# One input array in six transfers, the norm's weight folded into its scaling, and centering queued behind scaling, in a two-layer encoder

## The chip, the cores and the metric

The kernel runs on one core of one Trainium2 chip. The metric is the device time of that core in microseconds (us), launch to end. The median of three runs of the kernel before is 1676.47 us (1676.05 to 1679.31). Five engines work side by side and wait for each other through semaphores: PE (matmuls), DVE (vector), ACT (scalar), POOL (GpSimd) and SP, which here only issues transfers.

## The reference

Two layers on 256 tokens (272 in layer 0, with 16 learned tokens ahead) of width D = 1024, each a token mixer and a product-key expert layer, each followed by a residual sum and a layer norm:

```python
x = layer_norm(alpha * x + rglru_mixer(x))      # layer 0: x @ w_in, conv of 4 taps, gates, two scans, w_out
x = layer_norm(alpha * x + peer_ffn(x))
x = layer_norm(alpha * x + conformer(x))        # layer 1: pw1, GLU, conv of 31 taps, layer_norm, silu, pw2
x = layer_norm(alpha * x + peer_ffn(x))

def layer_norm(x, g, b):
    mu = mean(x); var = mean((x - mu) ** 2)
    return (x - mu) * rsqrt(var + eps) * g + b

def peer_ffn(x):                                # q = x @ w_query, top 16 of 2 x 128 keys, 16 experts of 16384
    ...                                         # weighted sum of expert rows peer_v by gelu(peer_u . x)
```

## The kernel before

**Layout.** Activations lie feature-major: a tile [128, 8, n] holds the 1024 features in 8 blocks of 128 partitions, n tokens along the free axis (n is 272 in layer 0 and 256 in layer 1). Weights come from memory in blocks of 512 KB, [128, 1024], into a ring "raw" of four buffers and at times a fifth (`stream`, `load` at L159, issued on SP's queue in program order; a counter `turn["raw"]`, modulo 5, says whose turn it is). For most products a weight block is split into a rounded high part (ACT, L172) and the rest (DVE, L181), and so are the activations; `linears` then makes three products for each block: high by high, low weight by high activation (on PE "u<-xs,lo"), and high weight by low activation. The first two blocks of a call can be held together (`defer=2`): for each k both units do the two products that need the activation's high part only, and the products that need its low part come last. `linears_whole` (L276) multiplies unsplit float32.

**The start.** `run` ends its setup with seven matmuls on a constant (L135, "idle"). `recurrent` (L466) then brings x and the first two blocks of w_in in eight transfers (L474 halves of a weight block, 256 KB; L478 quarters of x, 272 KB), then the parameter columns `par` (L480), one more block of w_in, and four blocks of gate weights (L506). The first two products (L608) run in halves of k: four k of unit 0, four of unit 1, and again. `gates(b)` makes the convolution of unit b on DVE (L508, then three L512), `uc`; PE multiplies it by the gate weights (L525, L527); meanwhile PE does the third unit of w_in (L276). Small DVE operations (L660 and others, "spl") make a softplus of 128x16 beside it.

**The norms.** `normed` (L399) is a generator: sums for mean and variance by matmuls with a constant matrix; centering x - mu on DVE (L405), 8 blocks; rstd by an ACT estimate and one Newton step of three DVE operations (L433 to L435), each of which needs the one before; scaling by rstd (L441), 8 blocks, each yielded to the caller. If products were made ahead (`self.pre` set), all 8 blocks are centered ahead of rstd; otherwise four are, and the other four are queued no earlier than L435. The norm inside the conformer (tile cy, 256 tokens) is the one of the second kind that the change touches; ACT applies weight, shift and silu (L1390), PE multiplies the first two weight blocks by cy unsplit (L223), and DVE splits cy for the rest (L1395, L1396).

**The norm ahead of the expert layer.** `norm_split` (L451), used once in each layer, writes for each block the high part `hi` = round(y*g + b) (ACT L457 for six blocks, POOL L455 for k = 2 and 5), then y = y*g + b in place (L462, six on DVE, two on POOL), then `lo` = y - hi (L463, DVE), and after blocks 3 and 7 a transfer of four blocks of y to memory ("saved", L671, on SP's queue). `peer` then takes the query products: q is written from two products made ahead (ACT L699) and from PSUM (DVE L701), in a tile that reuses the memory of x, so the first of these writes wait until "saved" has been read out of it. The products run over a ring of PSUM banks (0, 1, 2, 7, 6).

The order of the instructions on each engine is the program's, with a scheduler that places them by readiness; `issue_after(i)` holds an instruction of the same engine behind i.

## Time and profile before

| | |
|---|---|
| median of three runs | 1676.47 us (1676.05 to 1679.31) |
| profiled execution | 1678.47 us, span 1676.7 us, mean granted clock 0.998 |
| busy: PE, DVE, ACT, POOL | 1660.4, 1493.8, 1056.3, 744.1 us |
| PE's part of the chain that ended last | 94% |
| moved from and to memory | 449 MB, 268 GB/s over the span |

The profiled execution is 1.77 us longer than its span and 2.0 us above the median. A row of the timeline gives the start in us from the start of the span, the time from the first start to the last end of a group, the engine, the line, the operation with what it writes and reads, the number of instructions, and in brackets the idle time ahead of it with what ended it. Rows are modelled to overlap by a latency: eight matmuls of 0.23 us each take 2.00 us as a row, and the next row starts 1.83 us after the first.

### The profile page before, as it was taken

Reading aid. Unit: us, or ns where it says so; the run is one execution under the profiler, and the core shown is the slowest. Engines: PE = TensorE matmul, PEld = TensorE weight load, DVE = VectorE, ACT = ScalarE, POOL = GpSimd, SP = SyncE. Lnnn points to the kernel's source line nnn. Section 1 sums busy time; section 2 is a strip of 40 time slices with the busy share of each in tenths; the row PEclk is TensorE's granted clock in tenths of the full one; section 3 lists DMA queues with packets and bytes.
Section 4 is the critical chain, followed back from the end, with each engine's and each line's share of the span. In section 5 each row is a group of like instructions: output and inputs, shape, how many; then the busy total and the mean of one; then the engine's idle time right before and its main releaser. Section 6 shows DMA issues by size and latency. Waiting matters only on the chain.

```text
span 1676.7 us, 34167 instructions
## 1 busy us (share of the span) xinstructions
PE 1660.4 (99%) x12640; PEld 1609.8 (96%) x12640; DVE 1493.8 (89%) x2839; ACT 1056.3 (63%) x2024; POOL 744.1 (44%) x549
## 2 busy tenths in 40 slices
PE   9999999999999999999999999999999999999997
PEld 7999999999999999999989899999999999999997
DVE  6996999899998888988789969989899998899896
ACT  6754545578776555786567645456788875555552
POOL 0001873343453677753059017733333226777530
PEclk9999999999999999999999999999999999999999
DMA  6546679988777999999732355699888879999994
GB/s 214 176 158 172 201 222 357 315 287 282 258 263 238 350 345 354 347 357 333 272 113 89 126 178 185 210 320 335 289 290 269 280 239 354 356 374 362 366 369 159
DMA packets 135640, 451.17 MB, mean 269 GB/s; under 512 B 23472, under 2 KB 24624, under 8 KB 135344
## 3 DMA queue, kind: packets, MB, share of 16 engines
q1 hardware_dynamic: 98016, 324.66, 57.0%
q0 software_dynamic: 37456, 124.33, 20.2%
q8 instruction: 99, 1.62, 0.4%
q14 instruction: 69, 0.57, 0.1%
HBM read 437.10 MB, written 11.82 MB: 268 GB/s over the span
## 4 chain that ended last, share of the span: by engine, by line
PE 94%; DVE 4%; ACT 1%; issue 1%; DMA 0%; DVEq 0%; SPq 0%; ACTq 0%
PE u L215 32%; PE acc L935 20%; PE acc L939 13%; PE u L254 10%; PE u L257 5%; PE u L276 5%; PE g L841 1%; PE g L842 1%; PE cv L1518 1%; PE sps L716 1%; PE u L210 1%; PE acc L981 1%; PE u L608 1%; DVE lo L181 0%; PE pre L296 0%
## 5 line engine op out<-in xcount | busy, mean ns | idle before, releaser
L172 ACT ACTIVATE hi<-raw 128x1024 fp32r<-128x1024 f32 x559 | 592.0, 1060 | 481.9 <-PE acc L935 212.7
L181 DVE TENSOR_TENSOR lo<-raw,hi 128x1024 fp32r<-128x1024 f32 x503 | 616.4, 1227 | 98.7 <-ACT hi L172 96.5
L1270 POOL DMA_INDIRECT rows<-peer_v,ids x160 | 262.4, 1640 | 290.1 <-DVE few_out L1303 183.3
L215 PE MATMUL u<-xs,hi 128*128 128x240 f32 (+3 forms) x3056 | 385.9, 277 | 0.8 <-DVE xs L463 0.6
L935 PE MATMUL acc<-w,hi 128*128 128x384 f32 (+1 forms) x1952 | 374.1, 333 | 0.0
L215 PEld LDWEIGHTS u<-xs,hi 128*128 128x128 f32 x3056 | 364.5, 189 | 1.9 <-DVE xs L463 1.0
L935 PEld LDWEIGHTS acc<-w,hi 128*128 128x128 f32 x1952 | 320.1, 189 | 0.0
L939 PE MATMUL acc<-w,lo 128*128 128x192 f32 (+1 forms) x2016 | 261.2, 271 | 0.0
L939 PEld LDWEIGHTS acc<-w,lo 128*128 128x128 f32 x2016 | 258.8, 191 | 0.0
L215 PE MATMUL u<-xs,lo 128*128 128x240 f32 (+3 forms) x1528 | 208.8, 277 | 1.0 <-DVE lo L181 1.0
L1303 DVE SCALAR_TENSOR_TENSOR few_out<-rows,act,few_out 128x1024 f32<-128x1024 f32 x153 | 195.6, 1278 | 4.9 <-DMA rows<-peer_v,ids 4.9
L215 PEld LDWEIGHTS u<-xs,lo 128*128 128x128 f32 x1528 | 190.3, 189 | 1.5 <-DVE lo L181 1.4
L181 POOL TENSOR_TENSOR lo<-raw,hi 128x1024 fp32r<-128x1024 f32 x56 | 134.5, 2405 | 106.1 <-ACT hi L172 68.3
L254 PE MATMUL u<-xs,hi 128*128 128x448 f32 x784 | 179.5, 371 | 0.0
L1270 POOL DMA_INDIRECT rows<-u_rows,ids x64 | 88.2, 1379 | 170.7 <-DVE rows L1276 123.0
L1280 POOL DMA_INDIRECT act<-own,turn x96 | 139.9, 1458 | 40.3 <-issue 22.7
L254 PEld LDWEIGHTS u<-xs,hi 128*128 128x128 f32 x784 | 140.2, 189 | 10.3
L826 ACT ACTIVATE Bl<-AB,glT 128x128 f16<-128x128 f16 x368 | 112.8, 391 | 14.2 <-PE g L842 13.0
L257 PEld LDWEIGHTS u<-xs,lo 128*128 128x128 f32 x784 | 102.4, 191 | 3.4
L257 PE MATMUL u<-xs,lo 128*128 128x224 f32 x784 | 102.8, 273 | 0.0
L276 PE MATMUL u<-x,raw 128*128 128x272 f32 x368 | 86.6, 392 | 0.0
L276 PEld LDWEIGHTS u<-x,raw 128*128 128x128 f32 x368 | 69.9, 190 | 14.4
(332 smaller groups left out, 2016.4 us busy)
## 6 DMA issues: line engine op xcount, KB each, us to landing
raw<-peer_u SPq DMA_DIRECT2D x256, 512.0 KB, 4.7
raw<-peer_v SPq DMA_DIRECT2D x248, 512.0 KB, 6.3
raw<-w_query SPq DMA_DIRECT2D x28, 512.0 KB, 4.1
raw<-pw SPq DMA_DIRECT2D x22, 512.0 KB, 3.5
raw<-w_in SPq DMA_DIRECT2D x14, 512.0 KB, 5.2
own<-own POOLq DMA_DIRECT2D x20, 256.0 KB, 5.3
raw<-w_out SPq DMA_DIRECT2D x8, 512.0 KB, 3.3
raw<-peer_v SPq DMA_DIRECT2D x16, 256.0 KB, 4.1
```

The lines of the kernel that those rows point to most:

```text
L172: self.act_hi = nc.scalar.activation(hi, raw, AF.Copy).ins
L181: i = e.tensor_tensor(lo[:, s], raw[:, s], hi[:, s].bitcast(F32), op=OP.subtract)
L215: self.mm = nc.tensor.matmul(ps[:, :n], l[:, k, :], xs(k, r)[:, :n], start=start, stop=stop)
L254: self.mm = nc.tensor.matmul(both, hi[:, k, :], xs(k)[:, :, :n], start=k == 0, stop=k == NB - 1, skip_group_check=True)
L257: self.mm = nc.tensor.matmul(ps[:, n:2 * n], lo[:, k, :], xs(k, 0)[:, :n], start=False, stop=k == NB - 1, skip_group_check=True)
L276: self.mm = self.nc.tensor.matmul(ps[:, :n], raw[:, k, :], x[:, k, :n], start=k == 0, stop=k == NB - 1)
L826: nc.scalar.activation(Bl[:, c], Bh[:, c], AF.Copy, scale=glT[:, c0 + c:c0 + c + 1])
L935: self.mm = nc.tensor.matmul(acc[b][:, :2 * n], hi, w, start=j == 0, stop=j == NK - JG - 1, skip_group_check=True)
L939: self.mm = nc.tensor.matmul(main[b][:, :n], hi if p_ else lo, w[:, i * n:i * n + n], start=False, stop=j == NK - 1 and not p_, skip_group ...
L1270: self.last_rows = self.nc.gpsimd.indirect_dma_start(out=t, out_offset=None, in_=table, in_offset=bass.IndirectOffsetOnAxis(ap=few["ids"][ ...
L1280: self.nc.gpsimd.indirect_dma_start(out=few["act"][:, k:k + 1], out_offset=None, in_=few["lead"]["table"].rearrange("p j (t o) -> (p j t) ...
L1303: nc.vector.scalar_tensor_tensor(lead["out"], t, w, lead["out"], op0=OP.mult, op1=OP.add)
```

## The change

It has three parts.

1. **Start.** The host lays x and the first two weight blocks into one array "first", [128, 8, 272 + 256]: for each k the tokens and both units' 128 columns. Six transfers bring k = 0, 1, 2, 3 one by one (264 KB each), then 4-5 and 6-7 (528 KB each); `par` is issued ahead of the last. The two units' products follow the same bounds. The ring's counter is set to 2, so that the later loads use the same buffers as before. Five idle matmuls stand where there were seven. Gate blocks 0 and 2 are issued, then a block of w_in, then gate blocks 1 and 3. The scans write in place instead of in a tile of their own.
2. **norm_split.** The scaling multiplies by g and rstd in one operation on DVE (L443). `hi` takes only the shift and is made by ACT for all eight blocks (L457). `lo` = (y + b) - hi is one DVE operation (L461): eight where there were six and eight. y = y + b comes last and all on POOL (L464), each behind its own `lo`, and the two saving transfers behind the fourth and the eighth of these.
3. **Centering.** Where four blocks are centered after rstd, each is queued behind the scaling ahead of it instead of behind rstd.

```diff
+PARTS = (0, 1, 2, 3, 4, 6, 8)
...
-            for _ in range(7):
+            for _ in range(5):
                 nc.tensor.matmul(idle, self.ones16, self.ones16[:, None, :].to_broadcast([P, 4, P]), start=True, stop=True)
...
-    def normed(self, sp, y, n):
+    def normed(self, sp, y, n, gain=None):
...
-        i = nc.vector.scalar_tensor_tensor(r[1], r[1], 1.5, r[0], op0=OP.add, op1=OP.mult).ins
+        nc.vector.scalar_tensor_tensor(r[1], r[1], 1.5, r[0], op0=OP.add, op1=OP.mult)
         self.rstd = r[1]
         for k in range(NB):
             if k >= early:
-                with self.tc.issue_after(i):
+                with self.tc.issue_after(self.scaled):
                     center(k)
-            self.scaled = nc.vector.tensor_tensor(y[:, k, :n], y[:, k, :n], r[1], op=OP.mult).ins
+            z = y[:, k, :n]
+            self.scaled = (nc.vector.scalar_tensor_tensor(z, z, gain(k), r[1], op0=OP.mult, op1=OP.mult) if gain else
+                           nc.vector.tensor_tensor(z, z, r[1], op=OP.mult)).ins
             yield k
...
     def norm_split(self, sp, y, n, g, b, hi, lo, done):
         nc = self.nc
-        for k in self.normed(sp, y, n):
-            if k % 3 == 2:
-                nc.gpsimd.tensor_scalar(hi(k), y[:, k, :n], g(k), b(k), op0=OP.mult, op1=OP.add)
-            else:
-                i = nc.scalar.activation(hi(k), y[:, k, :n], AF.Identity, scale=g(k), bias=b(k))
-                if k == 7:
-                    self.pins.append(i.ins)
+        for k in self.normed(sp, y, n, g):
+            i = nc.scalar.activation(hi(k), y[:, k, :n], AF.Identity, bias=b(k))
+        self.pins.append(i.ins)
         for k in range(NB):
-            e = nc.gpsimd if k % 3 == 2 else nc.vector
-            e.tensor_scalar(y[:, k, :n], y[:, k, :n], g(k), b(k), op0=OP.mult, op1=OP.add)
-            nc.vector.tensor_tensor(lo(k), y[:, k, :n], hi(k).bitcast(F32), op=OP.subtract)
-            done(k)
+            z = y[:, k, :n]
+            i = nc.vector.scalar_tensor_tensor(lo(k), z, b(k), hi(k).bitcast(F32), op0=OP.add, op1=OP.subtract)
+        with self.tc.issue_after(i.ins):
+            for k in range(NB):
+                nc.gpsimd.tensor_scalar(y[:, k, :n], y[:, k, :n], b(k), None, op0=OP.add)
+                done(k)
...
+            first = sp.tile([P, NB, n + 2 * P], F32, name="first", bufs=1)
+            x = first[:, :, :n]
+            pair = [first[:, :, n + i * P:n + (i + 1) * P] for i in range(2)]
+            self.turn["raw"] = 2
+            for k, k1 in zip(PARTS, PARTS[1:]):
+                if k1 == NB:
+                    nc.sync.dma_start(self.par, a["par"])
+                nc.sync.dma_start(first[:, k:k1, :], a["first"][:, k:k1, :])
+            self.early.append(self.load(a["w_in"][0]))
...
-                    for i in range(4):
+                    for i in (0, 2, 1, 3):
+                        if i == 1:
+                            self.early.append(self.load(a["w_in"][1]))
                         nc.sync.dma_start(gw[:, i], a["gates"][i])
...
-                    h = sp.tile([P, n], F32, tag="h", name="h", bufs=4)
+                    h = t
...
-            for k0 in range(0, NB, 4):
+            for k, k1 in zip(PARTS, PARTS[1:]):
                 for t, raw in zip(ps, pair):
-                    for k in range(k0, k0 + 4):
-                        self.mm = nc.tensor.matmul(t, raw[:, k * P:(k + 1) * P], x[:, k, :], start=k == 0, stop=k == NB - 1)
+                    for i in range(k, k1):
+                        self.mm = nc.tensor.matmul(t, raw[:, i, :], x[:, i, :], start=i == 0, stop=i == NB - 1)
```

On SP's queue the kernel before starts with these transfers (x and h0, w_in's halves, par, then whole blocks):

```order
L474 DMA raw<-w_in 128x512
L478 DMA x_118<-h 128x544 x2
L474 DMA raw<-w_in 128x512 x2
L478 DMA x_118<-h 128x544 x2
L474 DMA raw<-w_in 128x512
L480 DMA par<-par 128x448
L159 DMA raw<-w_in 128x1024
L506 DMA gw<-gates 128x1024 x4
```

The changed kernel starts with these:

```order
L478 DMA first<-first 128x528 x4
L478 DMA first<-first 128x1056
L477 DMA par<-par 128x448
L478 DMA first<-first 128x1056
L160 DMA raw<-w_in 128x1024
L506 DMA gw<-gates 128x1024 x2
L160 DMA raw<-w_in 128x1024
L506 DMA gw<-gates 128x1024 x2
```

The first product needed two transfers, half a weight block and a quarter of x (528 KB), and needs one of 264 KB now; the fourth block of w_in has moved between the gate blocks.

On DVE, at the norm inside the conformer, the kernel before has this order (cy is the tile that is normed, mu its mean, L433 to L435 make rstd):

```order
L405 TENSOR_TENSOR cy<-cy,mu 128x256 x4
L433 SCALAR_TENSOR_TENSOR rstd_12104<-var,rstd_12103 128x256
L434 SCALAR_TENSOR_TENSOR rstd_12104<-rstd_12104,rstd_12103 128x256
L435 SCALAR_TENSOR_TENSOR rstd_12104<-rstd_12104,rstd_12103 128x256
L405 TENSOR_TENSOR cy<-cy,mu 128x256
L441 TENSOR_TENSOR cy<-cy,rstd_12104 128x256 x5
L405 TENSOR_TENSOR cy<-cy,mu 128x256 x2
L441 TENSOR_TENSOR cy<-cy,rstd_12104 128x256 x2
```

The changed kernel has this at the same place; the last two rows then come three times more:

```order
L406 TENSOR_TENSOR cy<-cy,mu 128x256 x4
L434 SCALAR_TENSOR_TENSOR rstd_12082<-var,rstd_12081 128x256
L435 SCALAR_TENSOR_TENSOR rstd_12082<-rstd_12082,rstd_12081 128x256
L436 SCALAR_TENSOR_TENSOR rstd_12082<-rstd_12082,rstd_12081 128x256
L444 TENSOR_TENSOR cy<-cy,rstd_12082 128x256 x4
L406 TENSOR_TENSOR cy<-cy,mu 128x256
L444 TENSOR_TENSOR cy<-cy,rstd_12082 128x256
```

No centering stands between rstd and the first scaling any more, and the later centerings alternate with the scalings of the same block.

On DVE, at the end of the norm ahead of layer 0's expert layer and at the first query products, the kernel before has this order (xs is the split activation, pre the products made ahead, lo a weight block's low part, q the queries):

```order
L462 TENSOR_SCALAR x_118<-x_118,par 128x272 x2
L463 TENSOR_TENSOR xs_1158<-x_118,xs_1158 128x272 x2
L310 COPY pre_c<-pre 128x2 x2
L312 SCALAR_TENSOR_TENSOR pre<-still,pre_c,pre 128x272 x2
L313 TENSOR_TENSOR pre<-pre,rstd_1188 128x272 x2
L181 TENSOR_TENSOR lo<-raw,hi 128x1024
L701 COPY q<-u 128x272 x2
L181 TENSOR_TENSOR lo<-raw,hi 128x1024
L701 COPY q<-u 128x272
```

The changed kernel has this, from the scaling on:

```order
L443 SCALAR_TENSOR_TENSOR first<-first,par,rstd_1166 128x272 x8
L461 SCALAR_TENSOR_TENSOR xs_1135<-first,par,xs_1135 128x272 x4
L461 SCALAR_TENSOR_TENSOR xs_1136<-first,par,xs_1136 128x272 x4
L311 COPY pre_c<-pre 128x2 x2
L313 SCALAR_TENSOR_TENSOR pre<-still,pre_c,pre 128x272 x2
L314 TENSOR_TENSOR pre<-pre,rstd_1166 128x272 x2
L182 TENSOR_TENSOR lo<-raw,hi 128x1024 x2
L701 COPY q<-u 128x272 x3
```

The six operations y*g + b have left DVE, and the first two copies to q, which wait for the saving transfers, stand behind a second weight block's low part.

More of the change, by code (lines that the diff above doesn't have):

```diff
@@ L469, in recurrent @@
         with tc.tile_pool(name="mix0", bufs=2) as sp:
-            x = sp.tile([P, NB, n], F32, name="x0", bufs=1)
-            pair = [self.stream("raw", F32, 4, None) for _ in range(2)]
-            def part(i, k):
-                nc.sync.dma_start(pair[i][:, k * P:(k + 4) * P], a["w_in"][i][:, k * P:(k + 4) * P])
-            for k in range(0, NB, 4):
-                part(0, k)
-                for k2 in (k, k + 2):
-                    nc.sync.dma_start(x[:, k2:k2 + 2, :], a["h0"][:, k2:k2 + 2, :])
-                part(1, k)
-            nc.sync.dma_start(self.par, a["par"])
-            self.early.append(self.load(a["w_in"][2]))
+            first = sp.tile([P, NB, n + 2 * P], F32, name="first", bufs=1)
[7 more added lines that the diff above has]
+            self.early.append(self.load(a["w_in"][0]))
             gw, pre_w = (sp.tile([P, 4, NB, P], F32, tag="gw", name="gw", bufs=1) for _ in range(2))
@@ L604, in recurrent @@
             ps = [self.psum("u", (0, 1, 2))[:, :n] for _ in pair]
-            for k0 in range(0, NB, 4):
+            for k, k1 in zip(PARTS, PARTS[1:]):
                 for t, raw in zip(ps, pair):
-                    for k in range(k0, k0 + 4):
-                        self.mm = nc.tensor.matmul(t, raw[:, k * P:(k + 1) * P], x[:, k, :], start=k == 0, stop=k == NB - 1)
+                    for i in range(k, k1):
+                        self.mm = nc.tensor.matmul(t, raw[:, i, :], x[:, i, :], start=i == 0, stop=i == NB - 1)
             for b in range(2):
                 gates(b, ps[b])
-            self.linears_whole([a["w_in"][b] for b in range(2, NB)], x, n, taken, (0, 1, 2))
+            self.linears_whole([a["w_in"][b] for b in range(NB - 2)], x, n, taken, (0, 1, 2))
             ring = (7, 0, 1, 2, 3, 4, 5, 6)
-            self.linears_whole([a["w_in"][NB + b] for b in range(WHOLE)], x, n, gelu, ring)
+            self.linears_whole([a["w_in"][NB - 2 + b] for b in range(WHOLE)], x, n, gelu, ring)
             self.hi_pin = last[0].ins
-            self.linears([a["w_in"][NB + b] for b in range(WHOLE, NB)], xs, n, FULL, lambda b, ps: gelu(WHOLE + b, ps), ring=ring)
+            self.linears([a["w_in"][NB - 2 + b] for b in range(WHOLE, NB)], xs, n, FULL, lambda b, ps: gelu(WHOLE + b, ps), ring=ring)
             for b in range(NB):
@@ L1681 @@
     arrays = {
-        "h0": np.ascontiguousarray(h0.reshape(T0, NB, P).transpose(2, 1, 0)),
+        "first": np.concatenate([h0.reshape(T0, NB, P).transpose(2, 1, 0),
+                                 *(w.reshape(P, NB, P) for w in w_in[NB:NB + 2])], axis=2),
         "par": np.ascontiguousarray(np.concatenate([cols(i[n]) for n, _ in _PARTS], axis=1)),
@@ L1685 @@
         "gb": np.stack([i["ln_ffn_g"][1], i["ln_ffn_b"][1]]),
-        "w_in": np.concatenate([w_in[NB:], w_in[:NB]]),
+        "w_in": np.concatenate([w_in[NB + 2:], w_in[:NB]]),
         "gates": np.ascontiguousarray(
```

## The prediction

> **What bounds the kernel now.** I read the page first, its busy times and its chain.
>
> ```profile
> span 1676.7 us, 34167 instructions
> PE 1660.4 (99%) x12640; PEld 1609.8 (96%) x12640; DVE 1493.8 (89%) x2839; ACT 1056.3 (63%) x2024; POOL 744.1 (44%) x549
> PE 94%; DVE 4%; ACT 1%; issue 1%; DMA 0%; DVEq 0%; SPq 0%; ACTq 0%
> ```
>
> PE is busy for all but 1676.7 - 1660.4 = 16.3 us, and it makes 94% of the chain. No product is removed except two idle ones, so a gain can only come out of PE's idle time at the places that the change touches. Next I read the timeline around those places: the start (four rows), then a narrow window at each norm (one row each).
>
> ```profile
> 1.14 3.17 PE L135 MATMUL idle<-ones 128*128 128x512 f16 x7 [1.14 <-POOL ones L108]
> 4.67 8.66 PE L608 MATMUL u<-x,raw 128*128 128x272 f32 x32 [0.36 <-DMA x<-h]
> 13.16 2.00 PE L276 MATMUL u<-x,raw 128*128 128x272 f32 x8
> ...
> 20.74 0.73 PE L527 MATMUL pi<-uc,gw 128*128 128x272 f32 x2 [0.54 <-ACT thi L532]
> 930.98 7.17 PE L223 MATMUL u<-cy,raw 128*128 128x256 f32 x32 [0.65 <-ACT cy L1390]
> 116.64 3.87 PE L215 MATMUL u<-xs,hi 128*128 128x272 f32 x28 [0.33 <-DVE xs L463]
> 969.98 3.69 PE L215 MATMUL u<-xs,hi 128*128 128x256 f32 x29 [0.25 <-DVE xs L463]
> ```
>
> PE waits 0.36 us for the first data and 0.54 us for a gate, 0.65 us for the first scaled block of the conformer's norm, and 0.33 and 0.25 us for the low parts after the norms ahead of the two expert layers. Together that is 2.13 us. The bound that a measurement of this kernel can tell from no change is about 0.2%, 3.35 us: even all of these waits together stay under it.
>
> **Part 1, the start.** The next rows are two matmul groups of narrow windows of the timeline, and, from the transfers' view of the first 14 us, the rate at which data came in (slices of 0.35 us from 0 on).
>
> ```profile
> 5.71 1.11 PE L608 MATMUL u<-x,raw 128*128 128x272 f32 x2
> 6.97 0.85 PE L608 MATMUL u<-x,raw 128*128 128x272 f32 x3
> GB/s 0 0 0 0 0 111 228 282 296 379 336 373 314 201 229 171 188 247 271 275 312 342 323 412 409 411 407 435 423 421 421 421 421 421 421 398 433 398 410 421
> ```
>
> The first product waited for 528 KB until 4.67; now 264 KB suffice. At the 296 to 379 GB/s of those slices 264 KB take about 0.8 us, so PE starts at about 3.9 instead of 4.67 (five idle matmuls of 3.17/7 = 0.45 us end at 3.4, so they are not in the way). But the first rows are slow: two in 1.11 us is 0.46 us from start to start, while from 6.97 on three in 0.85 is 0.23 (the overlap of 0.17 taken off). If the fast pace comes at the same moment as before, the 0.78 us of earlier start are worth half, 0.39 us, at the end of the 32 matmuls: 12.77 instead of 13.16. Then PE has the third unit, 16 matmuls of 0.23 us without a gate between them, until 16.4, and needs uc of unit 0.
>
> ```profile
> 11.53 0.56 DVE L508 TENSOR_SCALAR uc<-u,par 128x272 f32<-128x272 f32 x1
> ...
> 15.53 0.50 DVE L512 SCALAR_TENSOR_TENSOR uc<-u,par,uc 128x271 f32<-128x271 f32 x1
> 15.94 0.17 DVE L660 SCALAR_TENSOR_TENSOR spl_r<-spl_r,spl_q 128x16 f32<-128x16 f32 x1
> ```
>
> Both units now end together, so their convolutions alternate on DVE. Unit 1's first step starts at 12.9 and ends its slot at 13.4; then come five taps of 0.41 us with a small operation of 0.09 each until unit 0 is done: 15.9, at the latest 16.9. PE waits 0 to 0.5 us; I take 0.25. The gate wait of 0.54 us depends on ACT's chain behind uc; that chain starts about a microsecond later than now, so I count 0.40 of the 0.54 as coming back elsewhere. Sum: -0.39 + 0.25 - 0.54 + 0.40 = -0.28 us, between -0.9 (nothing comes back) and +0.4. The gate blocks' new order hides behind those three microseconds of products; if it did not, the 512 KB between them would cost 1.2 us at 420 GB/s.
>
> **Part 2, the norms ahead of the expert layers.** First layer 0, DVE and ACT, then POOL's two additions as a group, then what follows.
>
> ```profile
> 108.61 3.12 DVE L441 TENSOR_TENSOR x<-x,rstd 128x272 f32<-128x272 f32 x8
> 109.09 3.29 ACT L457 ACTIVATE xs<-x,par 128x272 fp32r<-128x272 f32 x6 [2.84 <-DVE x L441]
> 116.16 0.78 DVE L463 TENSOR_TENSOR xs<-x,xs 128x272 fp32r<-128x272 f32 x2
> 118.56 1.21 DVE L181 TENSOR_TENSOR lo<-raw,hi 128x1024 fp32r<-128x1024 f32 x1
> 119.70 0.78 DVE L701 COPY q<-u 128x272 f32<-128x272 f32 x2
> 125.83 1.16 PE L215 MATMUL u<-xs,lo 128*128 128x272 f32 x8
> L462 POOL TENSOR_SCALAR x<-x,par 128x272 f32<-128x272 f32 x2 | 1.6, 801 | 0.2
> ```
>
> DVE had 22 operations from 108.61 to 116.94; it has 16 now, of 0.39 us at most. The last low part is ready at 108.61 + 16 x 0.385 = 114.8 at the latest instead of 116.9. ACT makes eight high parts in place of six, 8 x 0.55 = 4.4 us from 109.09, 113.5, ahead of the last low part. So the wait of 0.33 us goes: -0.33. In layer 1 the same goes for 0.25: -0.25.
>
> What was added stands behind that: eight additions of p us each on POOL instead of two, the two saving transfers behind them, and behind those the first copies to q. In layer 1 the scaling, POOL's additions as a group, the saving transfer with its median from issue to landing, and PE's third group with a low weight part:
>
> ```profile
> 962.17 2.97 DVE L441 TENSOR_TENSOR x<-x,rstd 128x256 f32<-128x256 f32 x8
> L462 POOL TENSOR_SCALAR x<-x,par 128x256 f32<-128x256 f32 x2 | 2.2, 1084 | 0.2
> saved<-x SPq DMA_DIRECT2D x2, 512.0 KB, 2.8
> 978.48 1.12 PE L215 MATMUL u<-xs,lo 128*128 128x256 f32 x8
> ```
>
> POOL starts when the first low part is out, 8 scalings and one more operation of DVE behind 108.61, at about 111.95, and ends at 111.95 + 8p; the second transfer lands 2.8 us after its issue, 3.1 after the last addition. Then DVE has three copies (1.1 us) and the third low weight part (1.2 us), which PE needs at 125.83 - 0.33 - 0.1 for the weight load = 125.4: the copies must start by 123.1, so p up to (123.1 - 3.1 - 111.95)/8 = 1.01 us costs nothing. In layer 1 the same nine operations (0.34 us each there) let POOL start at 965.25; PE needs the part at 978.1, the copies must start by 975.9, and the bound is (975.9 - 3.1 - 965.25)/8 = 0.94 us. Of before's four additions two took 0.80 each and two 1.08 on average: I take p = 0.95 (their mean is 0.94), which costs nothing in layer 0 and 0.1 in layer 1. Ends: 0 at p = 0.80, 0.6 + 1.1 us at 1.08. On SP's queue the next query block stands behind the second transfer; six of these blocks are issued ahead of the transfers, so I cost that at nothing; a stall there would add to the stall on q.
>
> The Trainium skill (GPSIMD Engine Reference, section "When to use GPSIMD") puts one-input elementwise work on GpSimd at roughly line rate; the four additions agree only loosely, at 0.80 to 1.08 us against DVE's 0.39 us for the same block size.
>
> **Part 3, centering.** DVE's rows at the conformer's norm:
>
> ```profile
> 928.74 0.42 DVE L434 SCALAR_TENSOR_TENSOR rstd<-rstd,rstd 128x256 f32<-128x256 f32 x1
> 929.20 0.42 DVE L435 SCALAR_TENSOR_TENSOR rstd<-rstd,rstd 128x256 f32<-128x256 f32 x1
> ...
> 929.87 1.76 DVE L441 TENSOR_TENSOR cy<-cy,rstd 128x256 f32<-128x256 f32 x5
> ...
> 933.67 0.49 DVE L1395 CAST ch<-cy 128x256 fp32r<-128x256 f32 x2
> ...
> 949.74 1.21 PE L215 MATMUL u<-ch,lo 128*128 128x256 f32 x8
> ```
>
> Where an operation needs the one before it, starts are 0.46 apart (928.74 to 929.20); where not, (1.76 - 0.42)/4 = 0.335. The first scaling comes right behind L435 now: 929.66 instead of 929.87, and PE's first product 0.21 earlier. But then each of the four late blocks is centered and scaled back to back: 0.46 + 4 x 0.335 + 4 x (0.46 + 0.335) = 4.98 us from 929.20, so the casts start at 934.18 instead of 933.67, 0.5 later. Does PE feel it? From there to the low weight part that PE needs at 949.74 DVE runs without a gap: a window there has DVE at 1.00 of 1.00 and PE at 0.86.
>
> ```profile
> 949.00:950.00 1.00, 0.86 (x8) 0.66 (x7) 1.00 (x3) 1.00 (x4) 0.00 (x0) 1.00 0.00 0
> ```
>
> So PE, which already waits 0.14 us there, waits 0.5 more from the one shift and gains nothing from its earlier start: +0.48, between +0.5 and -0.2 (if DVE's order gives slack that I miss).
>
> The Trainium skill (VectorE: DVE Perf Modes, section "The DRAIN you can't avoid", and its rules for authors) says that a semaphore between chained DVE operations costs nothing extra and that only their number counts. The rows above disagree: 0.46 against 0.335.
>
> **Sum.** -0.28 - 0.33 - 0.25 + 0.10 + 0.48 = -0.28 us. The profiled execution would take 1678.47 - 0.28 = 1678.19 us; it was 2.0 us above the median of the runs, so the median comes to 1676.2 us.
>
> **The rivals.**
>
> *Dependent pairs cost nothing.* If starts are 0.335 us apart in any order, part 3 takes 13 x 0.335 = 4.36 us from 929.20: casts 0.11 us earlier, PE -0.11. With the start at its good end (-0.9) the sum is -0.9 - 0.33 - 0.25 - 0.11 = -1.6: 1674.9 us. That is the skill's rule on chained operations, worked out here; the rows quoted speak against it. 0.12.
>
> *POOL holds the queries: slower.* POOL's additions run beside a DVE that reads two tensors at every step, and 1.08 us is half of what was seen. With p = 1.1 the copies come 0.7 us late in layer 0 and 1.3 in layer 1: +2.0 on the rest, 1678.1 us; with p = 1.3 it is 2.3 + 2.9 = +5.2, 1681.3 us. It decides from p = 1.01 and 0.94. For it speaks the 1.08; against it the 0.80 twice beside a DVE that was busy all along. 0.14.
>
> *The fast pace comes later.* With five idle matmuls instead of seven, PE idles for about 0.5 us at 3.4. If the pace then changes only some 15 fast matmuls (3.4 us) later, 7.4 matmuls are done in that time at 0.46 us apiece that would take 1.7 us at 0.23: +1.7 on the rest, 1677.9 us. Before, 0.36 us of idling at 4.3 did not put it off. The Trainium skill (TensorE: Matmul & The Clock Gate, "What's actually happening") has the array start at half rate and be released after a busy window of 3.4 us that runs freely; the pace in the rows agrees, though their granted clock reads 1.00 throughout. 0.08.
>
> *The start gains nothing.* If small first transfers land no earlier (264 KB at the 111 to 228 GB/s of the first slices), the start's -0.28 turns into its bad end, +0.4, and the sum is -0.28 + 0.28 + 0.4 = +0.4: 1676.9 us, the change doing at the start not what it says. 0.08.
>
> **How the numbers follow.** The forecast, 1676.2 us, has 0.58 and its own range is 1675.2 to 1677.3. The range over all cases, 1674.2 to 1679.0 us, takes in the rivals but for the far ends of POOL's. Faster than 1673.1 needs more than the waits there are: 0.05, for what lies outside my terms. Slower than 1679.8 needs p of 1.2 or more, or two bad cases together: 0.08. Within 0.2%: 0.87.
>
> **What would show it.** L608 starts at 3.9 and the pair's products end near 12.8; PE has no wait for the low parts after the two norms; POOL's eight additions take under 0.95 us each and the copies to q run before 123.1 and 975.9 on before's clock; the casts of cy start 0.5 us later behind rstd than now, and PE waits about 0.6 us instead of 0.14 for the low part there. The forecast is wrong if POOL's additions last longer, if the conformer's norm does not lose, or if the time moves at a place not named here.

## The result, and the profile after

The changed kernel takes 1689.78 us (median of six runs, 1687.84 to 1691.03) against 1677.28 us for the kernel before, measured beside it (six runs). The ratio is 1.0073 (95% interval 1.006 to 1.0086): slower by some 12 us, where no change was forecast. The profiled execution took 1687.84 us, span 1686.1. It is the shortest of the six, and that of the kernel before was 2.0 us above its median, so the two spans differ by 9.4 us only.

The page's busy times and chain first:

```profile
span 1686.1 us, 34161 instructions
PE 1661.3 (99%) x12638; PEld 1611.8 (96%) x12638; DVE 1490.3 (88%) x2827; ACT 1058.0 (63%) x2028; POOL 753.1 (45%) x557
PE 87%; issue 7%; DVE 3%; POOL 1%; ACT 1%; DMA 0%; DVEq 0%; POOLq 0%; ACTq 0%
```

PE's busy time is the same within 1 us, but PE is idle for 1686.1 - 1661.3 = 24.8 us instead of 16.3. Where the time went is seen by following the same instructions in both traces:

| place (first or last start of a line's group) | before | after | shift |
|---|---|---|---|
| scaling, norm of layer 0 (L441, now L443) | 108.61 | 107.01 | -1.6 |
| first L716, behind layer 0's query products | 153.7 | 159.2 | +5.5 |
| first L841, ahead of the expert products | 345.2 | 350.7 | +5.5 |
| first L935, the expert products | 539.8 | 543.0 | +3.2 |
| scaling, norm of layer 1 | 962.17 | 965.73 | +3.6 |
| last L716, behind layer 1's query products | 1013.0 | 1023.5 | +10.5 |
| end of the span | 1676.7 | 1686.1 | +9.4 |

The start gains 1.6 us. Each of the two norms ahead of an expert layer then loses about 7 us. The conformer's norm lies between the fourth and the fifth row and loses 0.4. Together these places make -1.6 + 7.1 + 0.4 + 6.9 = 12.8 us, about what the medians differ by. The 2.3 us that the third and the fourth row win back, from 345 to 540 us, are no gain of the change: that stretch takes 194.6 us in this trace of the kernel before and 192.3 in that of the changed one, but 193.9 in the run "reverse" below, which repeats the changed kernel.

The next rows, from the timeline of layer 0, are one engine each: the last step of the norm on DVE, POOL's additions, the saving transfers' issue, the copies to q on DVE, and PE.

```profile
110.32 3.38 DVE L461 SCALAR_TENSOR_TENSOR xs<-first,par,xs 128x272 fp32r<-128x272 f32 x8
115.33 2.35 DVE L182 TENSOR_TENSOR lo<-raw,hi 128x1024 fp32r<-128x1024 f32 x2
110.91 12.23 POOL L464 TENSOR_SCALAR first<-first,par 128x272 f32<-128x272 f32 x8 [101.63 <-DVE xs L461]
119.40 4.15 SPq L671 DMA_DIRECT2D saved<-first  x2
126.67 1.14 DVE L701 COPY q<-u 128x272 f32<-128x272 f32 x3 [8.99 <-DMA saved<-first]
128.99 2.18 PE L216 MATMUL u<-xs,lo 128*128 128x272 f32 x8 [5.27 <-DVE lo L182]
130.96 3.61 PE L216 MATMUL u<-xs,hi 128*128 128x272 f32 x16
```

The low parts are done at 113.70, and the wait of 0.33 us that PE had for them is gone. But POOL's eight additions last 12.23 us, to 123.1; the second saving transfer lands at 126.6, as the chain of waits has it:

```profile
114.53 8.61 POOL first L464 x7
...
123.17 3.38 DMA saved<-first
```

DVE stands 8.99 us ahead of the copies to q; and the third low weight part, queued behind these, leaves PE idle for 5.27 us. The rows after that show a second cost: eight matmuls take 2.18 us where such a group took 1.16. The windows give the reason (busy PE is the third column, the granted clock the third from the end):

```profile
122.00:124.00 2.00, 1.72 (x14) 1.50 (x13) 0.00 (x0) 0.00 (x0) 1.14 (x2) 1.00 0.00 0
124.00:126.00 2.00, 0.00 (x0) 0.00 (x0) 0.00 (x0) 0.00 (x0) 0.00 (x0) 1.00 1.19 313
126.00:128.00 2.00, 0.00 (x0) 0.00 (x0) 1.33 (x4) 1.35 (x3) 0.00 (x0) 0.84 0.80 254
128.00:130.00 2.00, 1.01 (x4) 1.02 (x5) 2.00 (x3) 1.24 (x2) 0.00 (x0) 0.50 0.68 250
130.00:132.00 2.00, 2.00 (x11) 2.00 (x10) 1.21 (x3) 1.33 (x2) 0.00 (x0) 0.50 0.80 254
132.00:134.00 2.00, 2.00 (x11) 2.00 (x10) 0.78 (x1) 0.00 (x0) 0.00 (x0) 0.50 0.93 260
134.00:136.00 2.00, 2.00 (x17) 2.00 (x17) 0.39 (x2) 1.06 (x1) 0.00 (x0) 0.96 0.84 240
```

While PE is idle the granted clock falls to 0.50, and it stays there until about 134.2: PE works at half pace for 5.2 us and so loses another 2.6. Layer 1 repeats it, with 3.7 us at half pace:

```profile
969.56 11.72 POOL L464 TENSOR_SCALAR x<-x,par 128x256 f32<-128x256 f32 x8 [41.95 <-DVE xs L461]
984.97 1.09 DVE L701 COPY q<-u 128x256 f32<-128x256 f32 x3 [8.91 <-DMA saved<-x]
987.24 2.07 PE L216 MATMUL u<-xs,lo 128*128 128x256 f32 x8 [5.96 <-DVE lo L182]
```

The other two parts of the change, at the start and in the conformer's norm:

```profile
3.54 4.37 PE L608 MATMUL u<-first 128*128 128x272 f32 x16
8.14 3.97 PE L608 MATMUL u<-first 128*128 128x272 f32 x16 [0.23 <-DMA first<-first]
11.95 3.83 PE L277 MATMUL u<-first,raw 128*128 128x272 f32 x16
15.86 0.72 PE L525 MATMUL pr<-uc,gw 128*128 128x272 f32 x2
...
932.35 0.42 DVE L436 SCALAR_TENSOR_TENSOR rstd<-rstd,rstd 128x256 f32<-128x256 f32 x1
932.81 1.43 DVE L444 TENSOR_TENSOR cy<-cy,rstd 128x256 f32<-128x256 f32 x4
933.92 7.17 PE L224 MATMUL u<-cy,raw 128*128 128x256 f32 x32 [0.44 <-ACT cy L1390]
937.32 0.49 DVE L1395 CAST ch<-cy 128x256 fp32r<-128x256 f32 x2
953.30 1.21 PE L216 MATMUL u<-ch,lo 128*128 128x256 f32 x8 [0.38 <-DVE lo L182]
```

The first product starts at 3.54 instead of 4.67, the third unit at 11.95 instead of 13.16, and PE goes from it to the gates at 15.86 without an idle row. In the conformer's norm the first scaling stands 0.46 behind the last step of rstd, the casts 4.97 (before 4.47), and the products with the low weight part 20.95 (before 20.54).

### The profile page after: what moved, and what is told of

Its sections match the earlier page's. It is cut to its first block, busy times and chain, and to the rows that moved or that the text cites. A ratio compares the mean times of both kernels' runs of the same rounds, so it can differ in the third digit from the quotient of the medians.

```text
span 1686.1 us, 34161 instructions
## 1 busy us (share of the span) xinstructions
PE 1661.3 (99%) x12638; PEld 1611.8 (96%) x12638; DVE 1490.3 (88%) x2827; ACT 1058.0 (63%) x2028; POOL 753.1 (45%) x557
## 4 chain that ended last, share of the span: by engine, by line
PE 87%; issue 7%; DVE 3%; POOL 1%; ACT 1%; DMA 0%; DVEq 0%; POOLq 0%; ACTq 0%
PE u L216 29%; PE acc L935 20%; PE acc L939 13%; PE u L255 10%; PE u L258 5%; PE u L277 3%; PE g L841 1%; PE g L842 1%; PE cv L1518 1%; PE sps L716 1%; PE acc L981 1%; PE u L211 1%; DVE lo L182 1%; POOL first L464 1%; POOL x L464 0%
## 5 line engine op out<-in xcount | busy, mean ns | idle before, releaser
L182 DVE TENSOR_TENSOR lo<-raw,hi 128x1024 fp32r<-128x1024 f32 x503 | 615.7, 1226 | 100.4 <-ACT hi L173 97.6
L1270 POOL DMA_INDIRECT rows<-peer_v,ids x160 | 254.2, 1589 | 296.4 <-DVE few_out L1303 192.3
L935 PE MATMUL acc<-w,hi 128*128 128x384 f32 (+1 forms) x1952 | 374.1, 333 | 0.0
L935 PEld LDWEIGHTS acc<-w,hi 128*128 128x128 f32 x1952 | 320.0, 189 | 0.0
L216 PE MATMUL u<-xs,lo 128*128 128x240 f32 (+3 forms) x1528 | 210.6, 278 | 11.2 <-DVE lo L182 11.2
L182 POOL TENSOR_TENSOR lo<-raw,hi 128x1024 fp32r<-128x1024 f32 x56 | 134.4, 2401 | 99.7 <-ACT hi L173 65.2
L1276 DVE SCALAR_TENSOR_TENSOR rows<-rows,wide 128x1024 f32<-128x1024 f32 x64 | 77.9, 1217 | 2.5 <-DMA rows<-u_rows,ids 2.3
L464 POOL TENSOR_SCALAR first<-first,par 128x272 f32<-128x272 f32 x8 | 12.2, 1548 | 101.6 <-DVE xs L461 101.6
```

The costliest lines, as they stand in the source:

```text
L182: i = e.tensor_tensor(lo[:, s], raw[:, s], hi[:, s].bitcast(F32), op=OP.subtract)
L216: self.mm = nc.tensor.matmul(ps[:, :n], l[:, k, :], xs(k, r)[:, :n], start=start, stop=stop)
L935: self.mm = nc.tensor.matmul(acc[b][:, :2 * n], hi, w, start=j == 0, stop=j == NK - JG - 1, skip_group_check=True)
L1270: self.last_rows = self.nc.gpsimd.indirect_dma_start(out=t, out_offset=None, in_=table, in_offset=bass.IndirectOffsetOnAxis(ap=few["ids"][ ...
L1276: self.nc.vector.scalar_tensor_tensor(t, t, 1.0, few["x"], op0=OP.mult, op1=OP.mult, accum_out=few["act"][:, k:k + 1])
```

## The experiments

The theory after the first look: the loss comes from POOL's additions, through the saving transfers, the copies to q and the third low weight part, with the half pace behind the wait. Rivals were the wider array of x (its rows lie 528 elements apart), the order on DVE, and the transfers themselves. Times are medians; the kernel before ran beside each.

**The three parts, each alone.** `start` is the kernel before with the hunks of `recurrent`, the host arrays and the idle matmuls; `norm` with those of the scaling and of `norm_split`; `center` with this one:

```diff
-                with self.tc.issue_after(i):
+                with self.tc.issue_after(self.scaled):
                     center(k)
```

> The kernel before with the change's part 1 alone (one array in six transfers, five idle matmuls, gate order). Theory (POOL's additions make the loss): a gain of about 1.6 us, the lead that the changed kernel has at its first norm. Rival (the wider array, whose rows are 528 elements apart, slows the saving transfer of layer 0): slower by 1 us or more, PE with a wait after the first norm. My prediction had -0.3 us here.

> The kernel before with part 2 alone (weight in the scaling, one operation for the low part, additions on POOL). Theory: nearly the whole loss and more, +13 to +15 us, in two halves of about 7 us, one behind each norm, each of 5 to 6 us of idle PE and 2 to 2.5 us lost at half pace. Rival (the wider array matters): only the half of layer 1, about +7 us.

> The kernel before with part 3 alone (late centerings behind the scalings). As predicted for this part: +0.5 us, between -0.2 and +0.5; the casts of cy start 0.5 us later behind rstd and PE waits for the low weight part 0.4 to 0.6 us. A rival by which dependent operations cost nothing gives -0.1 us.

| | us | before | ratio, 95% interval |
|---|---|---|---|
| start | 1677.03 | 1677.73 | 0.9992 (0.9983 to 1.0001) |
| norm | 1691.35 | 1677.73 | 1.0076 (1.0062 to 1.009) |
| center | 1678.08 | 1677.73 | 1.0003 (0.9994 to 1.0012) |

Part 2 alone has the whole loss, 13.6 us, in both layers: PE waits 4.93 and 6.02 us behind the norms. There x has its old, compact tile, so the wider array is out. Part 1 is a small gain that the timing can't quite tell from nothing; part 3 is within the noise, and its trace repeats the 0.4 us (low weight part 20.94 behind rstd against 20.54). The three ratios add up to 1.0071, and the whole change has 1.0073.

**fold: the additions taken out.** The saved blocks lack the shift, and it is added where they are read back, in operations that are there anyway.

```diff
...
-        with self.tc.issue_after(i.ins):
-            for k in range(NB):
-                nc.gpsimd.tensor_scalar(y[:, k, :n], y[:, k, :n], b(k), None, op0=OP.add)
-                done(k)
+        for k in range(NB):
+            done(k)
...
-                    nc.scalar.activation(t, t, AF.Copy, scale=ALPHA)
+                    nc.scalar.activation(t, t, AF.Identity, scale=ALPHA, bias=self.alpha_b[:, b:b + 1])
...
-                summed = nc.vector.tensor_tensor(z[:, b, :], xr[b], main[b], op=OP.add).ins
+                summed = nc.vector.scalar_tensor_tensor(z[:, b, :], xr[b], self.col("ln_mix_b", NB + b), main[b], op0=OP.add, op1=OP.add).ins
```

> The changed kernel with POOL's eight additions taken out: the saved blocks hold the activations without the shift, and the shift is added where they are read back, as a bias of an existing ACT operation in layer 0 and as a scalar of an existing DVE addition in layer 1. The same output is computed. Theory: the whole loss goes, 13 to 15 us less than the changed kernel, and 1 to 2.5 us less than the kernel before; no PE wait over 0.3 us behind the norms. Rival (the order on DVE, three copies to q ahead of the third low weight part, or the saving transfers themselves): PE still waits several us behind the norms and the time stays above that of before.

1675.93 us against 1677.73, ratio 0.9988 (0.9979 to 0.9997): the whole loss is gone and a small gain is left. Behind the norms PE has no wait, and DVE none for the saving transfers:

```profile
113.51 4.19 PE L217 MATMUL u<-xs,hi 128*128 128x272 f32 x32
117.54 1.16 PE L217 MATMUL u<-xs,lo 128*128 128x272 f32 x8
116.43 0.78 DVE L702 COPY q<-u 128x272 f32<-128x272 f32 x2
```

So the loss goes with the additions, and the eight fused operations on DVE, which have stayed, don't make it. The order behind them has not stayed: one low weight part comes ahead of the first two copies to q now, where the changed kernel has two low weight parts and three copies. Whether the order counts is left to the next run.

**act: the additions on ACT.** Here they are still the last step of the norm, each behind its own low part, but on another engine.

```diff
-        with self.tc.issue_after(i.ins):
-            for k in range(NB):
-                nc.gpsimd.tensor_scalar(y[:, k, :n], y[:, k, :n], b(k), None, op0=OP.add)
-                done(k)
+        for k in range(NB):
+            nc.scalar.activation(y[:, k, :n], y[:, k, :n], AF.Identity, bias=b(k))
+            done(k)
```

> The changed kernel with the eight additions on ACT, behind the eight high parts there, instead of POOL. ACT's operation of this size has a pitch of 0.41 us, so the last addition ends at about 114.5 us in layer 0 instead of 123.1 and the saving transfers land before the copies to q are due. Theory: the loss goes but for 0 to 1 us (the weight blocks' high parts stand behind the additions on ACT): 12 to 14 us less than the changed kernel. Rival (that the additions stand last, behind every low part, is enough to hold q): the loss stays at 5 us or more.

1675.08 us against 1676.95, ratio 0.9987 (0.9978 to 0.9996). The eight take 3.40 us and the copies come at 118.25. The last three rows are from layer 1:

```profile
111.53 3.40 ACT L463 ACTIVATE first<-first,par 128x272 f32<-128x272 f32 x8
118.25 0.78 DVE L700 COPY q<-u 128x272 f32<-128x272 f32 x2
968.41 2.36 DVE L182 TENSOR_TENSOR lo<-raw,hi 128x1024 fp32r<-128x1024 f32 x2
970.69 1.31 DVE L700 COPY q<-u 128x256 f32<-128x256 f32 x3
971.92 1.22 DVE L182 TENSOR_TENSOR lo<-raw,hi 128x1024 fp32r<-128x1024 f32 x1
```

In layer 1 the order on DVE is that of the changed kernel, two low weight parts, three copies and the third low weight part, and PE has no wait behind either norm. So it is how long POOL takes that costs, not that the additions stand last, and the order alone makes no wait.

**reverse and late: why POOL takes 12 us.** `reverse` wrote the additions in the order 7 to 0.

> The changed kernel with POOL's additions in the order k = 7 to 0, so that the first of them waits for the last low part on DVE, 2.8 us later than in the changed kernel. Theory (an addition on POOL doesn't get on while DVE makes the low parts, two tensors and a scalar at each step; the first one's 3.6 us are mostly that): the first addition takes about 0.95 us, the last one ends no later than in the changed kernel, and the time is the same within 1 us or up to 3 us less, if the 1.2 us from start to start of the others shrinks to 0.95 without a wait of its own for each. Rival (an addition on POOL simply takes 1.5 us on average): POOL ends 2.8 us later and the time grows by 5 us over the two norms.

It tells nothing on that: the scheduler put them back in the order 0 to 7, and the run repeats the changed kernel (1691.27 us against 1676.95, ratio 1.009, 1.0075 to 1.0105; the first addition starts at 110.93 again). `late` holds the order:

```diff
-        with self.tc.issue_after(i.ins):
-            for k in range(NB):
-                nc.gpsimd.tensor_scalar(y[:, k, :n], y[:, k, :n], b(k), None, op0=OP.add)
-                done(k)
+        i = None
+        for k in reversed(range(NB)):
+            with self.tc.issue_after(i) if i else nullcontext():
+                i = nc.gpsimd.tensor_scalar(y[:, k, :n], y[:, k, :n], b(k), None, op0=OP.add).ins
+            if k % 4 == 0:
+                done(k + 3)
```

> The changed kernel with POOL's additions held in the order k = 7 to 0, so that the first waits for the last low part on DVE and the others need no semaphore from DVE (in layer 1 none at all). Theory (an addition on POOL doesn't get on while DVE makes the low parts): the first row takes about 0.95 us instead of 3.6, the others keep 0.95; in layer 1 the pitch falls from 1.2 to about 0.95 without semaphores, so POOL ends 1.5 to 2 us earlier there; the time is 1 to 4 us less than the changed kernel's. Rival (the first addition is long for a reason of its own, such as POOL's long idle time before it): the first row is 3.4 us again, POOL ends later than in the changed kernel in layer 0, and the time grows by 1 to 3 us.

1685.83 us against 1677.92, ratio 1.0045 (1.003 to 1.006), 4.7 us less than the changed kernel by the ratios. Narrow windows of POOL's timeline show single additions. The changed kernel, whose group "x8" is thus taken apart:

```profile
110.91 3.64 POOL L464 TENSOR_SCALAR first<-first,par 128x272 f32<-128x272 f32 x1 [101.63 <-DVE xs L461]
115.47 2.95 POOL L464 TENSOR_SCALAR first<-first,par 128x272 f32<-128x272 f32 x1
121.23 0.97 POOL L464 TENSOR_SCALAR first<-first,par 128x272 f32<-128x272 f32 x1
```

And late, with DVE's rows beside them and PE's first row behind the wait:

```profile
113.71 0.98 POOL L465 TENSOR_SCALAR first<-first,par 128x272 f32<-128x272 f32 x1 [104.51 <-DVE pre_c L311]
115.61 2.73 POOL L465 TENSOR_SCALAR first<-first,par 128x272 f32<-128x272 f32 x1
119.26 1.53 POOL L465 TENSOR_SCALAR first<-first,par 128x272 f32<-128x272 f32 x1
115.24 2.35 DVE L182 TENSOR_TENSOR lo<-raw,hi 128x1024 fp32r<-128x1024 f32 x2
118.73 1.23 DVE L182 TENSOR_TENSOR lo<-raw,hi 128x1024 fp32r<-128x1024 f32 x1 [1.14 <-ACT hi L173]
127.74 3.57 PE L216 MATMUL u<-xs,hi 128*128 128x272 f32 x16 [3.11 <-DVE q L703]
```

An addition takes 0.97 us. In the changed kernel two of the eight are longer: the first, which lies beside DVE's eight low parts (L461, until 113.70) and ends 0.85 us behind them, and the third, beside two low weight parts (L182, until 117.68), which ends 0.74 us behind those. In late the first starts behind the low parts and takes 0.98; the long rows are now the third and the fifth, and again they end 0.75 and 0.83 us behind L182. So of the changed kernel's 12.2 us about 8 x 0.94 = 7.5 are the additions' own (their starts are 0.94 apart where nothing holds them, 114.53 to 115.47), and 2.7 + 2.0 us they stand still until DVE's run is through. The rival, that the first is long for a reason of its own, falls. (The theory was wrong on one point: it expected gaps of 0.25 us between additions, for semaphores. There are none; the mean had hidden the second long row. So POOL ends no earlier in layer 1, at 981.42 against 981.28, where 1.5 to 2 us were expected.)

The 4.7 us don't come from POOL, whose last addition ends at 123.61 in layer 0, 0.5 us later than in the changed kernel. In late the third low weight part stands ahead of the copies to q (the row at 118.73), so PE waits for the first copy alone, 3.11 and 4.24 us in the two layers instead of 5.27 and 5.96. The order on DVE makes no wait by itself (act), but it adds to one that the transfers make.

**tt: which operation holds POOL.** The low part is made as y - hi, without the shift, which it then lacks.

```diff
-            i = nc.vector.scalar_tensor_tensor(lo(k), z, b(k), hi(k).bitcast(F32), op0=OP.add, op1=OP.subtract)
+            i = nc.vector.tensor_tensor(lo(k), z, hi(k).bitcast(F32), op=OP.subtract)
```

> The changed kernel with the low part as y - hi, an addition of two tensors without the scalar (the shift is left out of the low part). POOL's additions stay as they are. If the operation with two tensors and a scalar is what keeps POOL from getting on, the first addition takes 0.95 to 1.4 us, as POOL's high parts did in the kernel before beside DVE's scalings, and POOL ends about 2.5 us earlier; the third addition, beside two low weight parts on DVE, keeps its 2.9 us. If any operation of DVE that reads two tensors from SBUF does it, the first addition still takes about as long as DVE makes low parts, some 3 us.

One run, 1689.92 us against 1675.6. The first addition is held again:

```profile
111.01 3.22 POOL L464 TENSOR_SCALAR first<-first,par 128x272 f32<-128x272 f32 x1 [101.61 <-DVE xs L461]
```

It ends at 114.23, 0.85 us behind the low parts (110.48 + 2.90 = 113.38). So the scalar isn't needed for it; a run of operations that read two tensors is enough here. In the kernel before, two high parts of POOL beside DVE's L441 and L463, of the same kind, took only 1.41 and 1.15 us; why these weren't held for the whole run stays open.

**warm: what the half pace costs.** The changed kernel with idle matmuls in the wait.

```diff
...
                 for i in (0, 2, 1):
+                    if i == 1 and idx == 4 and warm:
+                        t = self.bank(5, "warm")
+                        for _ in range(warm):
+                            self.mm = nc.tensor.matmul(t, self.ones16, self.ones16[:, None, :].to_broadcast([P, 4, P]), start=True, stop=True)
                     for k in range(NB):
...
```

> The changed kernel with 22 idle matmuls (5 us at full pace) on PE just ahead of the products that wait for the third low weight part, once in each layer. Theory (after the wait PE works at half pace for 5.1 and 4 us): PE goes on at full pace and the time is 4 to 5 us less than the changed kernel's. Rival (the half pace is no cost of the wait, or other engines hold PE there anyway): the same time, or up to 1 us more where the idle matmuls outlast the wait.

1686.69 us, against 1691.27 for reverse in the same series, which repeats the changed kernel: 4.6 us less, as expected.

```profile
123.74 4.92 PE L269 MATMUL warm<-ones 128*128 128x512 f16 x22
130.01 1.26 PE L216 MATMUL u<-xs,lo 128*128 128x272 f32 x8 [1.34 <-DVE lo L182]
```

Behind the wait the eight matmuls take 1.26 instead of 2.18 us, and the granted clock stays at 1.00 in both layers. The wait itself is no shorter: with the idle matmuls in it it lasts 6.3 us in this trace against 5.3 (the last saving transfer took 4.23 us here and 3.38 in the changed kernel; why is open). So about a third of the loss, 4.6 of 14.3 us in this series, is the pace, and the rest the wait.

**six and four: fewer additions on POOL.** The rest goes to ACT.

```diff
-        with self.tc.issue_after(i.ins):
-            for k in range(NB):
+        for k in range(NB):
+            if k < 6:
                 nc.gpsimd.tensor_scalar(y[:, k, :n], y[:, k, :n], b(k), None, op0=OP.add)
-                done(k)
+            else:
+                nc.scalar.activation(y[:, k, :n], y[:, k, :n], AF.Identity, bias=b(k))
+            done(k)
```

In four the bound is `k < 4`.

> The changed kernel with the last two of the eight additions on ACT instead of POOL, six on POOL. Theory, by 1.2 us for each addition taken off: the copies to q start 2.4 us earlier, PE waits 2.9 and 3.6 us behind the norms instead of 5.3 and 6.0, and less is lost at half pace if these shorter waits don't lower the pace: 5 to 9 us less than the changed kernel. Rival (only the first, long addition matters): the same time as the changed kernel.

> The changed kernel with four additions on POOL (k = 0 to 3) and four on ACT. By 1.2 us for each addition POOL ends at about 118.2 us in layer 0, the first saving transfer lands at 121.5, about the time that my prediction's bound gives for the copies to q (123.1 on the clock of the kernel before, 1.6 us less here). Theory: PE waits 0 to 0.5 us in each layer, no half pace; the time comes within 1 us of that of the kernel with all additions on ACT. Rival (the bound is wrong, or the half pace comes after short waits too): 3 us or more above that.

Six: 1685.63 us against 1676.95, ratio 1.005 (1.0035 to 1.0065); PE waits 3.30 and 4.09 us, about as expected, and the pace falls all the same. Four: 1688.48 against 1677.92, ratio 1.0064 (1.0048 to 1.0079); waits of 3.19 and 3.97 us, where 0 to 0.5 was expected. Two pieces of four's chain of waits show why:

```profile
114.80 4.85 POOL first L464 x3
120.10 4.63 DMA saved<-first
```

The two long additions are both among the four, so POOL ends at 119.65 and not at 118.2; and the two transfers, now issued together and with the query blocks right behind, take 4.63 us, where the last one alone took 3.38. What four additions gain, the transfers give back.

**start7: where the start's gain comes from.** Part 1 alone with seven idle matmuls.

```diff
-            for _ in range(5):
+            for _ in range(7):
                 nc.tensor.matmul(idle, self.ones16, self.ones16[:, None, :].to_broadcast([P, 4, P]), start=True, stop=True)
```

> The kernel before with part 1 alone, but with its seven idle matmuls. The first 264 KB land at about 3.4 us; seven idle matmuls hold PE until 4.3. If the gain of the start comes from the earlier first product, the third unit starts 0.3 to 0.9 us later than with five idle matmuls (12.0 to 12.8 us over the runs so far). If it comes from the order of the products and gate blocks alone, the third unit's start moves but the first norm's scaling starts at 107.0 to 107.7 as with five.

```profile
4.10 8.03 PE L608 MATMUL u<-first 128*128 128x272 f32 x32
11.96 3.83 PE L277 MATMUL u<-first,raw 128*128 128x272 f32 x16
```

The first product starts 0.6 us later than with five (3.48 in start), yet the third unit starts at 11.96, no later than in the runs with five, and the first norm's scaling at 107.04, as with five. So in this run the number of idle matmuls made no difference. That speaks for the order of the data and of the products, but it isn't shown: this is one execution (1676.76 us), and where in the start PE's pace changes differs between executions by more than 0.6 us.

**fold_center: the best of the parts.** The fold, with the late centerings as in the kernel before.

```diff
...
-                with self.tc.issue_after(self.scaled):
+                with self.tc.issue_after(i):
                     center(k)
```

> The kernel with the shift folded into the read-back and the late centerings as in the kernel before; the best version by the theory. As the kernel with the fold alone less the 0.4 us of part 3: 1.5 to 3 us less than the kernel before. Rival (part 3 costs nothing): the same as the fold alone, about 1.8 us less than before.

1676.9 us against 1677.92, ratio 0.999 (0.9981 to 0.9999). It beats both kernels, but no more clearly than fold or act do; whether part 3 costs its 0.4 us the timing doesn't show.

## Why the prediction was wrong, point by point

The step that failed is in part 2: "I take p = 0.95 (their mean is 0.94), which costs nothing in layer 0 and 0.1 in layer 1." The price of one addition was right: 0.97 us in layer 0 and 0.92 in layer 1. What failed is the multiplication by eight. The additions stood still while DVE ran its low parts and low weight parts, 2.7 and 2.0 us in layer 0, so POOL ended at 110.91 + 12.23 = 123.1 instead of at 119.6 as 111.95 + 8 x 0.95 has it (118.0 on the clock of the changed kernel). Of these 5.2 us 4.7 are the standing still; the rest is a later start. The prediction had a row that warned of this, POOL's 1.08 us, and put it down to a slower p. The 1.08 us are a mean, as rows of the kernel before show when they are taken one by one:

```profile
964.64 0.85 POOL L462 TENSOR_SCALAR x<-x,par 128x256 f32<-128x256 f32 x1
966.16 1.32 POOL L462 TENSOR_SCALAR x<-x,par 128x256 f32<-128x256 f32 x1
966.13 1.07 DVE L463 TENSOR_TENSOR xs<-x,xs 128x256 fp32r<-128x256 f32 x3
```

The long one lies beside three operations of DVE that read two tensors. The Trainium skill (GPSIMD Engine Reference, section "1. Specifications") says that GpSimd shares its SBUF interfaces with VectorE, with contention when a VectorE instruction has two SBUF inputs. The long rows of after, late and tt agree, with 1.5 to 3.6 us where 0.97 is the free price; the prediction cited another section of that page and passed this one over.

**The bound itself held.** The copies were to start by 123.1 on the clock of the kernel before, 121.5 on that of the changed one. They started at 126.67, 5.2 us later, and PE waited 5.27.

**The landing was mis-sized.** The saving transfer was given 3.1 us behind the last addition and took 3.4 in the changed kernel. In four it landed 5.1 us behind POOL's last.

**The half pace was not priced.** The rival "POOL holds the queries" named the mechanism, with its place and its turning point; it had 0.14 and a price of 5.2 us at p = 1.3. By the same formula the effective 12.23/8 = 1.53 us in layer 0 and 11.72/8 = 1.47 in layer 1 give 4.2 + 4.2 = 8.4 us of waiting; the waits were 11.2 together. The half pace, for which the prediction had no term, added 2.6 + 1.8 us in the changed kernel's trace and 4.6 by the medians of warm and reverse. The Trainium skill (TensorE: Matmul & The Clock Gate, "What's actually happening") has the array fall back to half rate after an idle window of about 3.4 us. Here a wait of 3.1 us was enough (late, layer 0), and one of 1.34 left the pace alone (warm): close to the rule. The prediction had used that page for the start and not for its own slower rival.

How long a wait lasts says little, though, about how much the half pace then costs. Windows of 0.5 us, whose mean granted clock lies between 1.00 and 0.50 where it changes, give the moments for the fourteen waits of after, norm, reverse, late, six, four and tt. The clock fell 2.2 to 5.1 us after PE had become idle, three times only when it worked again, and came back either 3.41 or 6.83 us after its fall, each within 0.02.

**The start: right in sign, too small.** Forecast -0.28, shown -1.6 in the changed kernel's trace and -1.3 by the ratio of start, with an interval from -2.9 to +0.2. The pair's products ended 1.2 us earlier and not 0.39, the wait of 0.25 for uc didn't come, and nothing of the gate wait came back. One reason lies in the pace, which changed at 6.8 us in the kernel before and already at about 4.5 in the changed one. But it moves from run to run: in norm, with the start of the kernel before, the first four matmuls are at the full 0.23 us. In act and six, which have the changed start, it changes at about 7 us, as in the kernel before. There the third unit starts at 12.77 and 12.79, which is the forecast's 12.77, and the norm's scaling comes 0.9 and 1.1 us earlier than before. So the 0.39 us were right for an equal pace, the terms +0.25 and +0.40 were the wrong ones, and the other 0.5 to 0.7 us of the changed kernel's 1.6 came with the pace, by luck of the execution.

**The norms' own wait: right.** The 0.33 and 0.25 us for the low parts went, and the low parts ended 6.7 us behind the first scaling, as forecast (6.2) but for half a microsecond: the operations of the scaling and of the low part took 0.42 us from start to start where the sum has 0.385.

**The centering: right.** Forecast +0.48, shown +0.41 in the changed kernel's trace and +0.40 in center's; the times don't resolve it. Operations that need the one before stand 0.46 apart, others 0.34 (932.81: four in 1.43). The rival by which such pairs cost nothing falls.

**The sum.** Forecast -0.28 us, measured about +12. Without part 2's additions, in fold, it is -2.0 by the ratio (-3.5 to -0.5): the forecast's sign, and more than its size by what the start gained.

## What to carry to other kernels

Before work is moved to an idle engine, look at what runs beside it: a price read from rows beside one neighbour doesn't hold beside another, and eight operations aren't eight times one where some of them stand still. Follow the buffer as well: these additions were nobody's input, but the memory that they wrote was waited for by transfers, and the transfers by the copies that reuse it, and the copies had PE's next weights queued behind them. And price a wait of PE with what follows it: here waits of three microseconds or more cost about another 2 us each at half pace.

## What the runs showed of the hardware

POOL's one-input addition of 128x272 took 0.97 us beside an idle DVE or beside DVE operations with one operand in PSUM (L313, L314), and stood still beside runs of DVE operations that read two tensors from SBUF: 3.64 us beside eight of 128x272, 2.95 beside two of 128x1024, to 0.7 to 0.9 us behind the end of the run. Two other operations of POOL beside such runs took only 1.41 and 1.15 us (the kernel before), so when it is held is not fully known. The granted clock fell to 0.50 in waits of 3.1 to 6.0 us, or just behind them, and came back 3.41 or 6.83 us after its fall, which was 2.8 to 6.2 us after the work had begun again. At the start of the kernel the rows are at half pace while the granted clock reads 1.00, and the pace changed anywhere from 4.5 to 7 us in the traces of one and the same start.
